# SwiGLU on a 8192 x 8192 matrix: both one-row tiles moved to the end of the tile list

## The chip, the cores and the metric

The kernel runs on one core of a Trainium2 chip. The metric is the device time of one execution in microseconds (us), as the median of several runs. The execution that the profiler recorded has a time of its own, the span, which is a little shorter than the time of a run, because a run also counts what lies around the profiled instructions.

## What is computed

The input x is 8192 x 8192 in float32. Each row is cut into a left half a and a right half b, and the output, 8192 x 4096 in float32, is a times silu(b):

```python
a, b = np.split(x, 2, axis=-1)
silu_b = b / (1 + np.exp(-b))
return a * silu_b
```

So 268.44 MB are read and 134.22 MB are written, and each input element is used once.

## The kernel before

The 8192 rows are cut into tiles that cover all 128 partitions. A tile has one or two rows per partition: a one-row tile covers 128 rows of x (a load of 4096 KB and a store of 2048 KB), a two-row tile covers 256 (a load of 8192 KB and a store of 4096 KB). The list `rows` (line 26) sets the tiles: before, one row, then 31 tiles of two rows, then one row, 33 tiles in all with numbers 0 to 32 (`last` is 32).

There are three buffers, `slots` (line 32). Tile i lives in slot i % 3, and everything happens in place: the load fills the slot, ScalarE (ACT) overwrites b by silu(b) (line 62), VectorE (DVE) multiplies it with a and writes the product into the front of the slot (line 64), and the store sends the front of the slot to the output. The next load into the same slot, tile i + 3, waits until the store of tile i has landed.

The order is written out by hand (lines 83 to 97): loads 0, 1 and 2 are issued at once; then for each tile its arithmetic, its store, and the load of tile i + 3. Each engine carries out its own instructions in this order, which matters for SyncE (SP): it issues all 33 loads (line 51) and the last three stores, so its list ends with load 31, load 32, store 30, store 31, store 32. An instruction at the head of that list that waits holds back all behind it. The other stores (line 77) are issued by ACT, except stores 17 and 19, which GpSimd (POOL) issues (lines 74 to 76). Each issuing engine has its own DMA queue: q1 for SP, q10 for ACT, q0 for POOL. All three queues are served by the same 16 DMA engines, and each of the 16 carries 8 partitions of every transfer, one packet per partition: 64 KB for a two-row load, 32 KB for a one-row load or a two-row store, 16 KB for a one-row store.

The arithmetic of a tile is one ACT and one DVE instruction over both rows, with exceptions at the ends: `by_halves` (line 69) cuts a one-row tile into two halves of its columns (tiles 0 and 32), and tiles 1 and 31 are worked row by row (lines 88 to 90), so that DVE can begin on the first part while ACT does the second.

Of the kernel before, what the change touches and what calls it, by code (L numbers as in the profile page):

```python
# [1 line left out]

# [4 lines left out]

_SILU = mybir.ActivationFunctionType.Silu


@with_exitstack
def kernel(
    ctx: ExitStack,
    tc: tile.TileContext,
    x: bass.AP,
    out: bass.AP,
):

    nc = tc.nc  # L20
    N, M = x.shape
    half = M // 2
    P = nc.NUM_PARTITIONS
    BUFS = 3

    rows = [1] + [2] * (N // P // 2 - 1) + [1]
    first = [sum(rows[:i]) * P for i in range(len(rows))]
    last = len(rows) - 1

    pool = ctx.enter_context(tc.tile_pool(name="sbuf", bufs=1))  # L30
    ctx.enter_context(tc.manual_schedule())
    slots = [pool.tile([P, 2 * M], x.dtype, name=f"slot{s}") for s in range(BUFS)]
    loads, gates, prods, stores = ([[] for _ in rows] for _ in range(4))
    newest = {}

    def in_dram(t, i, width):

        return bass.AP(t.tensor, first[i] * width, [[rows[i] * width, P], [1, rows[i] * width]])

    def follows_from_others(inst, i, current, earlier):  # L40


        targets = [t for kind in current for t in kind[i]]
        targets += [t for kind in earlier for j in range(i % BUFS, i, BUFS) for t in kind[j]]
        for t in targets:
            if t is not newest.get(inst.ins.engine):
                tc.declare_no_dep(inst.ins, t.ins, reason="ordered by the other waits")
        newest[inst.ins.engine] = inst

    def load(i):  # L50
        inst = nc.sync.dma_start(  # L51
            out=slots[i % BUFS][:, : rows[i] * M], in_=in_dram(x, i, M)
        )
        follows_from_others(inst, i, [], [loads, gates, prods])
        loads[i].append(inst)

    def swiglu(i, k0, k1, c0=0, cw=half):
        view = slots[i % BUFS].rearrange("p (k s c) -> p k s c", k=2, s=2)
        a = view[:, k0:k1, 0, c0 : c0 + cw]
        b = view[:, k0:k1, 1, c0 : c0 + cw]  # L60
        o = slots[i % BUFS][:, : 2 * half].rearrange("p (k c) -> p k c", k=2)
        gate = nc.scalar.activation(out=b, in_=b, func=_SILU)  # L62
        follows_from_others(gate, i, [], [loads, gates, prods, stores])
        prod = nc.vector.tensor_mul(out=o[:, k0:k1, c0 : c0 + cw], in0=a, in1=b)  # L64
        follows_from_others(prod, i, [loads], [loads, gates, prods, stores])
        gates[i].append(gate)
        prods[i].append(prod)

    def by_halves(i):
        for c0 in range(0, half, half // 2):  # L70
            swiglu(i, 0, 1, c0, half // 2)

    def store(i):
        eng = nc.scalar if i < last - 2 else nc.sync
        if i % 2 and last // 2 <= i < last // 2 + 4:
            eng = nc.gpsimd
        inst = eng.dma_start(  # L77
            out=in_dram(out, i, half), in_=slots[i % BUFS][:, : rows[i] * half]
        )
        follows_from_others(inst, i, [loads, gates], [loads, gates, prods, stores])  # L80
        stores[i].append(inst)

    for i in range(BUFS):
        load(i)
    for i in range(last):
        if i == 0:
            by_halves(i)
        elif i in (1, last - 1):
            swiglu(i, 0, 1)
            swiglu(i, 1, 2)  # L90
        else:
            swiglu(i, 0, rows[i])
        store(i)
        if i + BUFS <= last:
            load(i + BUFS)
    by_halves(last)
    store(last)


# [1 line left out]
_INS = ['x']  # L101
_OUTS = [((8192, 4096), 'float32')]


# [23 lines left out]
```

## Time and profile before

| | |
|---|---|
| median of 3 runs | 934.87 us (934.86 to 935.44) |
| span of the profiled execution | 933.16 us, so 1.71 us of the median lie outside it |
| DVE, ACT busy | 278.7 us, 226.8 us |
| mean DMA rate over the span | 432 GB/s |
| tile 0: load landed, store issued | 12.93 us, 19.42 us |
| tile 32: load landed, store issued, store landed | 908.10 us, 915.45 us, 932.28 us |

Times in the trace are counted from the start of the span. "Issued" is when an engine hands a DMA to its queue, "landed" is when the last of the 16 DMA engines has reported it done. The trace also holds a record for each packet: queue, start, duration and size. The number of the DMA engine is not in the record, but the packets of one engine follow each other so closely that they can be strung together.

### The profile page before, as it was taken

How to read it: one execution, taken by the hardware profiler on the slowest of the kernel's cores; microseconds unless marked ns; L12 is line 12 of the kernel's file. 1: busy time of each engine (PE TensorE's matmuls, PEld its weight loads, DVE VectorE, ACT ScalarE, POOL GpSimd, SP SyncE). 2: the span in 40 equal slices, each digit the busy share in tenths (PEclk: the TensorE clock that was granted, in tenths of full speed). 3: DMA queues.
4: the chain of work that ended last, by engine and by line, in shares of the span. 5: the costliest groups of instructions: out<-in, count | busy, mean ns of one | idle time of the engine just before them, and what ended most of it. 6: DMA issues, size and time to landing. Idle time of an engine off the chain costs nothing.

```text
span 933.2 us, 220 instructions
## 1 busy us (share of the span) xinstructions
DVE 278.7 (30%) x37; ACT 226.8 (24%) x38; POOL 1.4 (0%) x6
## 2 busy tenths in 40 slices
DVE  1312333123331233312333113332133321333242
ACT  2331133311333203332033320233202332023330
POOL 0000000000000000000000000000000000000000
DMA  9999999999999999999999999999999999999998
GB/s 405 405 449 431 423 451 444 409 444 433 444 427 434 442 410 448 428 433 442 434 421 441 445 417 444 428 454 427 420 457 405 449 427 428 448 445 409 427 444 388
DMA packets 9505, 402.67 MB, mean 432 GB/s; under 512 B 1056, under 2 KB 1056, under 8 KB 1056
## 3 DMA queue, kind: packets, MB, share of 16 engines
q1 hardware_dynamic: 5184, 278.92, 69.1%
q10 hardware_dynamic: 4032, 115.35, 28.6%
q0 software_dynamic: 288, 8.39, 2.1%
q14 instruction: 1, 0.01, 0.0%
HBM read 268.44 MB, written 134.22 MB: 431 GB/s over the span
## 4 chain that ended last, share of the span: by engine, by line
DMA 72%; DVE 11%; ACT 8%; issue 6%; another core or an unknown queue 1%; DVEq 0%; POOL 0%; SPq 0%; ACTq 0%; POOLq 0%
DMA slot<-in_x_dram 40%; DMA out_dram<-slot 32%; DVE slot L64 11%; ACT slot L62 8%; DVEq L123 0%; POOL out_dram L77 0%; SPq L51 0%; ACTq L77 0%; DVEq L64 0%; POOLq L123 0%
## 5 line engine op out<-in xcount | busy, mean ns | idle before, releaser
L64 DVE TENSOR_TENSOR slot<-slot 128x8192 f32<-128x8192 f32 (+2 forms) x37 | 278.7, 7539 | 636.7 <-ACT slot L62 636.5
L62 ACT ACTIVATE slot<-slot 128x8192 f32<-128x8192 f32 (+2 forms) x37 | 225.6, 6107 | 684.3 <-DMA slot<-in_x_dram 684.3
L77 POOL DMA_DIRECT2D out_dram<-slot x2 | 1.2, 600 | 568.9 <-DVE slot L64 568.9
L62 ACT ACT_TABLE_LOAD x1 | 1.3, 1283 | 0.7 <-PEq L112 0.7
L112 POOL MEMSET const-bfloat16-1.0<- 128x1 bf16 x1 | 0.1, 102 | 0.0
L112 POOL MEMSET const-float32-0.0<- 128x1 f32 x1 | 0.1, 99 | 0.2 <-issue 0.2
L112 POOL MEMSET const-float32-1.0<- 128x1 f32 x1 | 0.1, 99 | 0.0
L112 POOL MEMSET const-uint8-127<- 128x1 uint8 x1 | 0.1, 99 | 0.0
## 6 DMA issues: line engine op xcount, KB each, us to landing
out_dram<-slot ACTq DMA_DIRECT2D x27, 4096.0 KB, 33.5
slot<-in_x_dram SPq DMA_DIRECT2D x2, 4096.0 KB, 13.6
out_dram<-slot POOLq DMA_DIRECT2D x2, 4096.0 KB, 34.4
out_dram<-slot SPq DMA_DIRECT2D x2, 4096.0 KB, 20.4
out_dram<-slot ACTq DMA_DIRECT2D x1, 2048.0 KB, 28.1
out_dram<-slot SPq DMA_DIRECT2D x1, 2048.0 KB, 16.8
slot<-in_x_dram SPq DMA_DIRECT2D x31, 37.7
```

The source lines that it names most:

```text
L62: gate = nc.scalar.activation(out=b, in_=b, func=_SILU)
L64: prod = nc.vector.tensor_mul(out=o[:, k0:k1, c0 : c0 + cw], in0=a, in1=b)
L77: inst = eng.dma_start(out=in_dram(out, i, half), in_=slots[i % BUFS][:, : rows[i] * half])
L112: nc = _bacc.Bacc("TRN2", target_bir_lowering=False, num_devices=1)
```

## The change

The list of tiles becomes 31 tiles of two rows followed by two tiles of one row. The number of tiles stays 33, and so do the slot of each tile number, the engine that issues each load and store, and the waits between them. Tile 0 becomes a two-row tile and is worked row by row instead of by halves; tiles 1 and 2 stay as they are in size; tile 30, still of two rows, is worked row by row instead of in one instruction; tile 31 has one row and is worked in one instruction; tile 32 stays a one-row tile by halves. Each tile from 1 to 31 begins 128 rows later in x. ACT and DVE carry out 37 instructions of arithmetic each, before and after: 29 of 128x8192, 4 of 128x4096 and 4 of 128x2048 elements before; 28, 7 and 2 after.

```diff
-    rows = [1] + [2] * (N // P // 2 - 1) + [1]
+    rows = [2] * (N // P // 2 - 1) + [1, 1]
     first = [sum(rows[:i]) * P for i in range(len(rows))]
     last = len(rows) - 1
...
     for i in range(last):
-        if i == 0:
-            by_halves(i)
-        elif i in (1, last - 1):
+        if i in (0, 1, last - 2):
             swiglu(i, 0, 1)
             swiglu(i, 1, 2)
         else:
```

## Prediction, made before the result was known

> **What bounds the kernel now.** I read first the page's totals and its 40 slices.
>
> ```profile
> span 933.2 us, 220 instructions
> ## 1 busy us (share of the span) xinstructions
> DVE 278.7 (30%) x37; ACT 226.8 (24%) x38; POOL 1.4 (0%) x6
> ...
> DMA  9999999999999999999999999999999999999998
> ...
> DMA packets 9505, 402.67 MB, mean 432 GB/s; under 512 B 1056, under 2 KB 1056, under 8 KB 1056
> ```
>
> DVE and ACT work for under a third of the span, while the DMA engines are busy in every slice, the first and the last too. Next, the table of stretches, for the time between the first packet and the last:
>
> ```profile
> core 0: us, DVE busy (x) ACT busy (x) POOL busy (x), PEclk, DMA share, GB/s
> 2.00:932.00 930.00, 278.68 (x37) 225.58 (x38) 1.20 (x2) 1.00 1.00 432
> ```
>
> The DMA share is 1.00 over 930 us. Strung together by engine, the packet records confirm it: the first starts at 1.74 us, the last ends at 931.95, and between them the 16 engines together show one pause above 0.03 us, of 0.34. The span is therefore 1.74 us of start, 930.2 us of DMA engines at work without a hole, and 1.2 us behind the last packet. What matters is that packets are never lacking, not when a given tile is computed.
>
> Third, the end, where a hole could open. The chain of waits, from store 28 on, and SP's instructions in order of time:
>
> ```profile
> 830.95 33.04 DMA out_dram<-slot
> 863.98 0.02 issue
> 864.00 34.39 DMA slot<-in_x_dram
> 898.39 0.02 issue
> 898.41 3.63 ACT slot L62
> 902.04 0.02 issue
> 902.06 4.44 DVE slot L64
> ```
>
> ```profile
> 864.00 29.33 SPq L51 DMA_DIRECT2D slot<-in_x_dram  x2
> 893.38 22.40 SPq L77 DMA_DIRECT2D out_dram<-slot  x3
> ```
>
> Store 28 lands at 863.98 and load 31 follows, landing at 898.39. In SP's rows the second load, load 32, is issued at 893.00 (864.00 + 29.33, less the 0.33 it takes), when store 29 has landed (892.98). The three stores behind it run from 893.38 to 915.78. Store 30's product was ready at 888.85 (DVE: 880.16 + 8.69); it stood 4.5 us behind the waiting load. That cost nothing, as load 31 still had packets in q1.
>
> **The change part by part.**
>
> *Bytes and packets.* Per DMA engine both kernels carry 31 x 8 load packets of 64 KB (2.418 us each), 2 x 8 of 32 KB (1.213), 31 x 8 store packets of 32 KB (1.213) and 2 x 8 of 16 KB (0.611): 599.7 + 19.4 + 300.8 + 9.8 = 929.7 us, plus some 0.6 us of end markers. The change orders them anew; their sum changes by 0.
>
> *Arithmetic.* DVE goes from 29 x 8.692 + 4 x 4.426 + 4 x 2.286 = 278.9 to 28 x 8.692 + 7 x 4.426 + 2 x 2.286 = 278.9, ACT likewise. Nothing changes, and with a third of the span busy it would stay hidden.
>
> *The start.* Load 0 is 4096 KB more, 8 packets per engine of 2.418 instead of 1.213: its landing goes from 12.93 to 12.93 + 9.64 = 22.6. Tile 0 then takes 3.6 (ACT, first row) + 2 x 4.43 (DVE) + 0.1 = 12.6 instead of 6.5, so store 0 is issued at 35.2 instead of 19.42. The cover is the three loads queued at once, now 24 packets of 2.418 per engine, which last until 1.74 + 0.7 + 58.0 = 60.4 even without store 0. That store enters some 1 us after its issue (the first load: issued 0.74, first packet 1.74) and one packet further on, near 38.7. From there its 8 packets alternate with load packets, 2.418 + 1.213 = 3.63 us a pair, and end near 67.7; load 3 is issued near 69. Load 2 lasts until 71.4, and store 1 has stood in q10 since 56 (load 1 landed at 43.3, plus 12.6). Neither queue runs dry: 0 us. If this cover failed, load 3 would miss some 2 us.
>
> *The phase that the start leaves.* When a store has ended on an engine, the next load enters only after landing, semaphore and issue; I count how many packets of the load before it are left then. In the trace of before it is 3 or 4 at first, 2 from 196 us on, and 3 from 571 us on, where the POOL store's later entry gave loads a free turn. In the changed kernel it starts at 1: store 1 ends near 96.8 and load 3 near 100.4. The stores have more lead in return: store 2 is issued at 88, 9 us before store 1 lands (4.5 before). So POOL's stores 17 and 19 can run beside the ACT store ahead of them, which ends each of them a turn earlier against the loads, and the count should rise by about one at either. I take 2 to 3 at the end and keep 1 as a bound.
>
> *The end.* Before, one engine does this: store 28 ends at 861.17; three pairs end load 30 at 872.06; five store packets alternate with five of load 31; store 29 ends at 890.20; three 64 KB packets, 7.25 us, are left until 897.45. After, load 31 has 32 KB packets, so the alternation is one to one. With count c, 8 - c packets of each pass in turn after load 30, and c packets of 1.213 us remain when store 29 ends there: cover 3.64, 2.43 or 1.21 us for c = 3, 2, 1. Against it stands the turnaround to load 32's first packet. Engines end store 29 within 0.6 us of each other (890.17 to 890.79) but for one, 2.43 later, half of which is 1.21 with the smaller packets; landing follows the last marker by 0.35, SP's issue by 0.02, the first packet by 1.0. That is 2.0 us without a late engine, 2.6 with one. The hole is then 0 (c = 3), 0 to 0.2 (c = 2), 0.8 to 1.4 (c = 1); restarting after a pause costs 0.7 more, by the first packets of the kernel (1.9 instead of 1.213). So 0, 0 to 0.9, or 1.5 to 2.1 us. The restart after so short a pause is not in the trace: between 0 and 0.7 (nothing makes it a gain), I take half for a near miss.
>
> Behind load 32 no hole follows. Store 30 is in q1 at once and brings 9.7 us more work. One-row tile 31 needs 3.62 + 4.43 = 8.1 us from its landing, at most 2 us before load 32 starts, and has 19.4 us of packets as cover. Tile 32 needs 1.9 + 4.6 = 6.5 from its landing, with store 30 and store 31 (9.7 + 4.85) as cover. The last store is 16 KB packets as before, and 1.2 us follow.
>
> *Sum.* 0 (bytes) + 0 (start) + 0 to 0.9 (end) makes 933.2 to 934.1 for the span; I take 933.4. With the 1.7 us outside the span: 935.1, against a median of 934.87.
>
> **A rule weighed.** Row: two filled queues alternate record by record, 64 KB, 32 KB, 64 KB (861.18, 863.59, 864.81). The Trainium skill, "DMA: Bandwidth & Descriptors", section "Queues, rings and completion order", says an engine drains a whole packet of typically 9 to 17 descriptors from one queue before it switches. If that packet were a transfer's whole share, load 31 could be gone before store 29 ends; the trace disagrees for these transfers.
>
> **The rivals.**
>
> 1. *A hole behind store 29* (slower). SP can't issue store 30, ready before store 29 lands, past the waiting load 32, so only load 31's rest fills the engines. It decides from a count of 1 with a late engine: 2.1 us, 937.0. For it: the start gives 1, and one engine is late in most of before. Against it: the POOL stores raise the count, and the phase before was at 3 here. Chance 0.13.
> 2. *Queues drained transfer by transfer* there: load 31 leaves no cover, so the full turnaround of 2.0 and a restart of 0.7 are lost: 2.7, 937.5 (the rule above would do this). Against it: the alternation in all of before. Chance 0.03.
> 3. *Fill decides*: the chain of waits moves with tile 0's later landing, 9.6 us: 944.5. Against it: no DMA pause in 930 us. Chance 0.02.
> 4. *A shorter drain* (faster). After the last load only 4096 + 2048 + 2048 KB of stores are left instead of 10240 KB, 2048 KB or 4.85 us less: 930.0. Against it: the same bytes are then moved earlier on engines with no idle time to take them. Chance 0.03.
>
> That the change doesn't do what it says is excluded by the built order of instructions: tile 0 is 128x16384 elements, tiles 31 and 32 are 128x8192, and the waits are the same.
>
> **How the numbers follow.** The forecast, with count 1 and no late engine (1.5 us, 936.4) counted in, has 0.79; the rivals have 0.13, 0.03, 0.02 and 0.03. A measurement can tell about 0.2%, 1.9 us. Faster: rival 4, 0.03. Slower: rivals 1 to 3, 0.18. Same: 0.79. The range reaches from 934.3 (the forecast less the spread of the runs) to 937.2 (rival 1); rivals 2 to 4 are left out.
>
> **What would show it.** Right: DMA share 1.00 from 2 to 932 us, load 0 landing near 22.6, store 0 issued near 35, store 30 issued right behind load 32, the last store landing at 932 to 933. Rival 1: a pause in q1 on most engines between load 31's last packet and load 32's first, and a last landing shifted by just that. Wrong altogether: 64 KB packets longer than 2.418 us somewhere, or a pause in the first 100 us.

## The result, and the profile after

The changed kernel takes 938.29 us (median of 15 runs, 935.27 to 939.95), the kernel before 935.23 us in the same comparison (15 runs, 934.86 to 937.32). The ratio is 1.0026 with a 95% interval of 1.0018 to 1.0033: slower by 0.26%, some 2.4 us by the ratio and 3.1 by the medians. It lies above the predicted range. The profiled execution took 937.14 us, 1.15 less than the median, with a span of 935.4 against 933.16 before. First its page:

```profile
span 935.4 us, 221 instructions
## 1 busy us (share of the span) xinstructions
DVE 278.9 (30%) x37; ACT 226.8 (24%) x38; POOL 1.4 (0%) x6
...
DMA  9999999999999999999999999999999999999998
...
DMA packets 9505, 402.67 MB, mean 430 GB/s; under 512 B 1056, under 2 KB 1056, under 8 KB 1056
```

The number of packets, the bytes and the busy time of the engines are what they were; only the mean rate fell, from 432 to 430 GB/s. The table of stretches for the time between the first packet and the last (columns as before) looks almost harmless:

```profile
2.00:934.00 932.00, 278.87 (x37) 225.52 (x38) 1.20 (x2) 1.00 1.00 431
```

The DMA share is again 1.00, now over 932 us instead of 930. A share of 1.00 therefore does not say that no time was lost: a packet's record mostly runs on until the next one begins (the two times agree within 0.01 us), so a pause can hide inside a longer packet. I compared each packet's length with what its size usually takes (2.414, 1.209 or 0.607 us from start to start) and added up the excess, as a mean over the 16 engines:

| where | before | after | what stands there |
|---|---|---|---|
| first packet | 0.76 | 0.70 | start of the kernel |
| 20 to 45 us | 0.73 | 1.36 | load 1's packets while store 0, the first transfer in q10, enters |
| 900 to 915 us | 0 | 1.46 | load 32 |
| last packet's end, first and last engine | 931.33, 931.95 | 933.15, 934.15 | |

So 1.46 us were lost at the end and 0.6 more than before at the start; the latest engine, which lags the mean a little more, adds 0.1. That makes the 2.2 us between the two spans. The rest of the 3.1 us between the medians lies in executions slower than the profiled one, which this trace doesn't show. The chain of waits shows the end (start, length, what):

```profile
875.25 26.07 DMA out_dram<-slot
901.32 0.02 issue
901.34 13.76 DMA slot<-in_x_dram
915.10 0.02 issue
915.12 1.92 ACT slot L62
917.04 0.02 issue
917.07 2.29 DVE slot L64
```

Store 29 is issued at 875.25 and lands at 901.32; 0.02 us later load 32 goes out, and lands after 13.76 us. Before, load 31 stood in this place; load 32 lay behind it in a filled queue. SP's instructions in order of time:

```profile
879.58 22.09 SPq L51 DMA_DIRECT2D slot<-in_x_dram  x2
901.72 20.20 SPq L77 DMA_DIRECT2D out_dram<-slot  x3
```

Load 32 and store 30 are issued 0.38 us apart, as before. What differs is the queue at that moment. One engine's packets in q1 (KB at start, in us; s is a store packet of q10, | the end marker of a transfer):

```
before  887.78 64 | s-end 890.20  890.20 64  892.62 64  895.03 64 | 897.45 32  898.66 32 ...  905.92 32 | 907.13 32
after   899.04 32 | s-end 900.25  900.25 32  901.46 32 | 902.68 32  904.05 32 ...  910.10 32  912.00 32 | 914.02 32
```

On this engine, before, load 31 still had 7.25 us of packets when store 29 ended, and load 32 was issued (893.00) 4.45 us before they ran out. After, it had 2.43 us, and load 32 came (901.34) only 1.34 us before the queue was dry. Its first packet then took 1.37 us, and its last two 1.90 and 2.01 instead of 1.21. Over the 16 engines the first packet lost 0.25 us and the last two 1.21: the greater part of the loss does not stand where the queue ran dry, but 7 to 9 us behind it.

### The profile page after: what moved, and what is told of

It is laid out like the page before. It is cut to its first block, busy times and chain, and to the rows that moved or that the text cites. A ratio compares the mean times of both kernels' runs of the same rounds, so it can differ in the third digit from the quotient of the medians.

```text
span 935.4 us, 221 instructions
## 1 busy us (share of the span) xinstructions
DVE 278.9 (30%) x37; ACT 226.8 (24%) x38; POOL 1.4 (0%) x6
## 4 chain that ended last, share of the span: by engine, by line
DMA 78%; DVE 10%; ACT 8%; another core or an unknown queue 2%; DVEq 0%; issue 0%; SPq 0%; ACTq 0%
DMA slot<-in_x_dram 41%; DMA out_dram<-slot 37%; DVE slot L64 10%; ACT slot L62 8%; DVEq L121 0%; SPq L51 0%; ACTq L77 0%; DVEq L64 0%
## 5 line engine op out<-in xcount | busy, mean ns | idle before, releaser
L64 DVE TENSOR_TENSOR slot<-slot 128x8192 f32<-128x8192 f32 (+2 forms) x37 | 278.9, 7539 | 642.7 <-ACT slot L62 642.4
```

## The experiments

Theory A: the loss at the end comes from q1 running dry while load 32 waits for store 29, and some 0.6 us come from the start. Rivals: the start costs everything (B), the turn from loads to stores in one queue costs it, or the shifted rows do (C). All times are medians, each set against the kernel before measured again beside it.

**e1, the changed kernel again.**

> The changed kernel once more, for a second profile. Theory A (a hole at the end, before load 32, plus some 0.6 us at the start) and rival B (the start costs it all) both expect about 938.3 us. A expects in the trace packet time lost around 901 to 914 us, 1.5 us or more, in every execution, and more of it in a slower one; B expects the end whole and the loss in the first 50 us.

938.25 us (937.17 to 938.86) against 935.07, ratio 1.0027 [1.0018, 1.0037]. The second profile has the same places: 1.2 us at 35 to 45 us, 1.51 us at 902 to 914. One engine ends at 935.06 while most others end near 933.4, so the span is 936.3 instead of 935.4: the latest engine sets the time. B falls.

**e2, no wait: tile 32 in the free half of tile 31's slot.**

```diff
+    def slot(i):
+        return i % BUFS if i < last else (last - 1) % BUFS
+    def base(i):
+        return 0 if i < last else M
...
-            out=slots[i % BUFS][:, : rows[i] * M], in_=in_dram(x, i, M)
+            out=slots[slot(i)][:, base(i) : base(i) + rows[i] * M], in_=in_dram(x, i, M)
```

(and the same places in the arithmetic and the store of tile 32)

> Tile 32 is loaded into the free upper half of tile 31's slot, so load 32 no longer waits for store 29 and is issued right behind load 31. A: the hole at the end goes, the start's 0.6 us stay: 935.4 to 936.4 us. B: the start is untouched, so the time stays near 938.3. C (the last packets of a load stall whenever a store follows them in the same queue): 0.3 us better at most, 938.

936.31 us (935.95 to 936.87), ratio 1.0007 [0.9997, 1.0016]. Nearly 2 of the 3 us are gone. SP's rows:

```profile
879.62 0.87 SPq L57 DMA_DIRECT2D slot<-in_x_dram  x2
901.14 19.60 SPq L87 DMA_DIRECT2D out_dram<-slot  x3
```

Both loads are now issued within 0.87 us, store 30 as late as ever. No packet from 880 us on is longer than its size says, although loads are followed by stores in q1 as in the changed kernel. The turn from loads to stores is not the cause; the wait on a queue about to run dry, which this edit takes away, can be. What is left, 1.2 us by the medians (the interval of the ratio just takes in no difference) and 1.0 by the spans, stands at 36 to 45 us: a mean of 1.46 us, and up to 2.1 on three engines.

**e3, store 30 on ScalarE's queue.**

```diff
-        eng = nc.scalar if i < last - 2 else nc.sync
+        eng = nc.scalar if i < last - 1 else nc.sync
```

> Store 30 is issued by ScalarE on its own queue instead of by SyncE behind load 32; load 32 still waits for store 29. A: the short pause before load 32's first packet stays (some 0.3 us), the loss at the handover from load 32 to store 30 goes, since the two queues alternate: about 937. B: no change, 938.3. C: the handover is gone, 937.

939.88 us, ratio 1.0043 [1.0027, 1.0059]: slower than the changed kernel itself, which none of the three expected. All instructions from 895 us on:

```profile
901.17 0.33 SPq L51 DMA_DIRECT2D slot<-in_x_dram  x1
901.38 0.34 ACTq L77 DMA_DIRECT2D out_dram<-slot  x1
...
912.52 18.74 SPq L77 DMA_DIRECT2D out_dram<-slot  x2
924.45 3.71 ACT L62 ACTIVATE slot<-slot 128x2048 f32<-128x2048 f32 x2 [16.42 <-DMA slot<-in_x_dram]
```

Store 30 had waited only some 0.3 us behind load 32 (its product is ready at about 901.05). On a queue of its own it shares the engines with load 32, which lands at 924.43 instead of 915.10; store 32 is issued at 930.9, and the engines stand idle for 3.7 us between the end of store 31 and it. Load 32 loses 1.0 us in its first two packets here and nothing in its last ones. So store 30 behind load 32 in SP's list is not the fault: taken out of it, the kernel is slower.

**e4, the end alone.**

```diff
-    rows = [2] * (N // P // 2 - 1) + [1, 1]
+    rows = [1, 1] + [2] * (N // P // 2 - 2) + [1, 1]
...
-        if i in (0, 1, last - 2):
+        if i == 0:
+            by_halves(i)
+        elif i in (2, last - 2):
```

> Two one-row tiles at each end (34 tiles): the end has the sizes of the changed kernel, the start is as light as before. A: the end's loss without the start's: 1.5 to 2.5 us over the kernel before, 936.7 to 937.7. B: the start is light, so no loss: 934.5 to 935.5.

938.57 us (935.72 to 941.18), ratio 1.0027 [1.0012, 1.0043]. Without the heavy first load the loss at the end is there, 1.6 us at 902 to 914, so B fails again. The time overshoots what A expected: in its profile one engine ends 2 us behind most others, and it has been behind since 103 us, so this run bears out A by its trace more than by its time.

**e5, the wait covered: store 30 in two rows, one of them ahead of load 32.**

```diff
+        if i == last - 2:
+            swiglu(i, 0, 1)
+            store_row(i, 0)
+            load(last)
+            swiglu(i, 1, 2)
+            store_row(i, 1)
+            continue
```

> Store 30 is cut into its two rows, and the first one (2048 KB, 4.85 us of packets) is issued by SyncE ahead of load 32, which still waits for store 29. A (the loss at the end comes from queue q1 running dry while load 32 waits): the wait stays and is covered, so about the time of the half-slot run, 935.9 to 936.9 us. Rival (the loss belongs to the turn from loads to stores in one queue): there are more such turns, so 938.3 or more.

936.84 us, ratio 1.0016 [1.0007, 1.0025]. SP's rows:

```profile
879.59 0.33 SPq L51 DMA_DIRECT2D slot<-in_x_dram  x1
896.66 0.35 SPq L84 DMA_DIRECT2D out_dram<-slot  x1
901.35 0.33 SPq L51 DMA_DIRECT2D slot<-in_x_dram  x1
901.77 0.43 SPq L84 DMA_DIRECT2D out_dram<-slot  x1
```

Load 32 waits just as long (901.35), but 2048 KB of a store (4.85 us) lie ahead of it: the excess at the end falls from 1.46 us to 0.05 (the half microsecond over e2 goes with one engine that ends 1.5 us behind most others). The same loss was removed in two ways, by taking the wait away and by covering it: the wait on a dry queue is its cause.

**e6, a lighter start on top of e2.** Tile 0's load and store are cut into rows:

```diff
+    load_row(0, 0)
+    load_row(0, 1)
...
+    swiglu(0, 0, 1)
+    store_row(0, 0)
+    swiglu(0, 1, 2)
+    store_row(0, 1)
```

> The half-slot kernel (no wait of load 32 on store 29), and tile 0's load and store are each cut into two rows, so that the first row lands near 12.9 us and its product is stored near 21. A with a start loss from the late first store: both losses gone, 935.0 to 935.5 us. Rival (the rest of the loss comes from the shifted rows, or from somewhere in between): 936.3, as with the half slot alone.

937.10 us, ratio 1.0016 [1.0007, 1.0025]: no gain. The pauses at 20 to 45 us are 1.03 us instead of 1.46, but the two small stores take until 72.76 to land, load 3 waits for both, q1 runs dry near 70.5, and 1.0 us is lost at 75 to 83. The edit brought in the fault that it was to show the absence of; on the start it decides nothing.

**e7 and e8, no store from GpSimd**, in the changed kernel and in the one before:

```diff
-        if i % 2 and last // 2 <= i < last // 2 + 4:
-            eng = nc.gpsimd
```

> The changed kernel with stores 17 and 19 issued by ScalarE instead of GpSimd. A: the count of load packets left when a store ends stays at 1 up to the end instead of rising, so load 32's wait finds 1.2 us less cover: 939 to 940.5 us. Rival (GpSimd's stores have no part in it): 938.3.

> The kernel before, with stores 17 and 19 issued by ScalarE. A: the count stays at 2, the cover before load 32 is 2 packets of 64 KB, 4.8 us, against a turnaround of up to 3.8: no hole, 934.7 to 935.4 us. Rival (the GpSimd stores by themselves cost or save time): outside that.

e7: 937.83 us (937.68 to 938.52), ratio 1.0026 [1.0015, 1.0037]. SP's rows:

```profile
881.83 20.93 SPq L51 DMA_DIRECT2D slot<-in_x_dram  x2
902.81 20.31 SPq L75 DMA_DIRECT2D out_dram<-slot  x3
```

In the trace A's step is there: one load packet instead of two is left at the end of store 29, load 32 is issued at 902.43, 0.45 us before the queue is dry, and the loss grows from 1.46 to 2.45 us. The span is 936.6, against 935.4 and 936.3 for the changed kernel. The step is all in load 32's first packet (1.34 us instead of 0.25); its last two lose 1.1 as ever. The median, though, is not higher, so the price in time was not confirmed; the scatter of the latest engine is as large as the effect. e8: 935.25 us, ratio 0.9999 [0.9991, 1.0008], as A expected.

**e9, tile 30 in one piece.**

```diff
-        if i in (0, 1, last - 2):
+        if i in (0, 1):
```

> The changed kernel with tile 30 worked in one ACT and one DVE instruction instead of row by row, so store 30 is ready at about 904.2 us, 2.9 us behind load 32's issue instead of 0.38. Theory A1 (the second pause, in load 32's last packets, comes from two DMAs handed to a dry queue back to back): the first pause stays, the second goes, about 937.0 us. Rival A2 (it follows from load 32 entering a dry queue, whatever comes behind it): 938.3 as the changed kernel.

937.88 us, ratio 1.0024 [1.0015, 1.0034]. Store 30 is issued at 904.83, 3.7 us after load 32, and the pauses are the same two, 0.27 and 1.16 us. A1 falls: it is not the closeness of the two issues. Working tile 30 by rows costs and brings nothing that can be seen.

**e10, the kernel before on shifted rows.**

```diff
-    first = [sum(rows[:i]) * P for i in range(len(rows))]
+    first = [N - P] + [sum(rows[1:i]) * P for i in range(1, len(rows))]
```

> The kernel before with its first tile taken from the last 128 rows of x and every other tile 128 rows earlier, so that tiles 1 to 31 work on the very rows that tiles 0 to 30 have in the changed kernel; sizes, order and waits are those of before. A: rows don't matter, 934.8 to 935.5 us. Rival C (the shifted rows cost the rest that the half slot left): about 936.3.

935.23 us, ratio 0.9999 [0.9990, 1.0008], and the pauses of before (0.65 at 20 to 35 us, none at the end). C falls: which rows a tile holds does not matter.

**e11, q10 used before store 0**, on top of e2:

```diff
+    warm = pool.tile([P, 128], x.dtype, name="warm")
+    nc.scalar.dma_start(out=warm[:, :], in_=bass.AP(x.tensor, 0, [[M, P], [1, 128]]))
```

> The half-slot kernel, and ScalarE issues one small load (64 KB in all, into a tile that nothing reads) at the very start, so that queue q10 has been used before store 0 comes. Theory S1 (the start's pause is the first use of q10): the pause at 36 to 45 us shrinks, about 935.6 us. Rival S2 (any queue that takes up work after being empty pauses the engines, and a light first use doesn't help): 936.3, as the half-slot kernel alone.

935.93 us (935.62 to 936.47), ratio 0.9998 [0.9986, 1.0011], against e2's 1.0007 [0.9997, 1.0016]; by the medians it is 0.7 us above the kernel before, e2 1.2. The pause at 36 to 45 us is 0.95 us instead of e2's 1.46. That points to S1, but weakly: the intervals overlap, the same start shows anything from 1.06 to 1.46 us in seven profiles (after, e1, e2, e3, e5, e7, e9), and 0.95 is still above the 0.64 to 0.73 of the start of before (before, e8, e10). It is a part of the start's cost at most.

**e12, e2's end with e4's start.**

> The half-slot end with two one-row tiles at the start instead of a two-row one (34 tiles). Against the end-alone run only the wait of load 32's successor on a store is gone; against the half-slot run only the start is lighter. A (a hole at the end and a heavier start, each on its own): both are gone, 935.0 to 935.8 us. Rival (the sizes at the end cost time even without the wait): 936.3 or more.

936.69 us (935.08 to 940.40), ratio 1.0013 [0.9999, 1.0027]. In the profile no packet at the end is longer than usual and the pauses of the start are 0.6 us; 13 of the 16 engines end by 931.7, as before, but the last at 933.4. One lagging engine again sets the time. The pauses went as A expected, but the median did not: it is in the rival's range. The rival's reason does not fit the trace, though. The late engine fell behind in mid-run, from 0.5 to 1.5 us behind the median engine between 190 and 395 us, long before the small tiles at the end. What costs e12 its time is not settled.

## Why the prediction was wrong

*Bytes, packets, arithmetic: 0.* Right. Packets, bytes and DVE's 278.9 us are as forecast.

*The start: 0.* The course was right: load 0 landed at 22.60 (forecast 22.6), store 0 was issued at 35.26 (35.2), load 3 at 69.62 (near 69), and q1 did not run dry. But the entry of store 0 was costed as a change of place alone. In the trace 1.36 us are lost there against 0.73 before, on average and more on some engines; 1.21 of the 1.36 stand in load 1's last packet, and so do 0.58 of the 0.73. The 0.73 was in the trace of before, hidden in the lengths of packets, where a search for pauses between records could not find it. e2, which leaves the start alone, still has a span 1.0 us above before's. Part of it may go when q10 has been used before (e11); why the rest is larger than before was not settled.

*The count of packets left: 1 at the start, raised by GpSimd's stores to 2 to 3.* Right: near 97 us one packet is left on 13 of the engines and two on three, at the end two on 13 and three on three, and e7 shows that without those stores it stays at one on most. Of before the prediction read one engine only: on 12 or more of the 16 the count was three from store 1 to the end, not two.

*The end: a hole of 0 to 0.9, and behind load 32 no hole.* The first half held; the second is the step that failed. The place, the cover (2.43 us) and the landing were as forecast, and so, nearly, was the turnaround. I took 1.0 us from issue to first packet and 0 to 0.7 for the restart. If a packet's start is counted as its end less its usual length, load 32's first packet began 1.8 to 2.1 us after the issue (the mean, in each profile of the table, over the engines on which it was late). The kernel's first load has the same figure, 1.9 us from issue, so the 0.7 belonged into the sum in full. With 1.9 the prediction's own sum for a count of two is 0.6 + 0.35 + 0.02 + 1.9 - 2.43 = 0.4 us; 0.25 was lost. But for what follows the sum had nothing. Load 32's last two packets took 1.2 us longer than usual, and store 30's packets began late by as much:

| run | load 32 issued | load 31's last packet ends (mean) | lost in load 32's first packet | lost in its last two |
|---|---|---|---|---|
| after | 901.34 | 903.06 | 0.25 | 1.21 |
| e1 | 901.29 | 902.90 | 0.33 | 1.22 |
| e4 (loads 33, 32) | 901.13 | 902.64 | 0.40 | 1.27 |
| e7 | 902.43 | 902.97 | 1.34 | 1.12 |
| e9 | 901.11 | 902.95 | 0.27 | 1.18 |

e7 parts the two. Its queue had 0.5 us left at the issue instead of 1.7, and the first loss grew by 1.1 us, as the prediction's mechanism has it; the second stayed. Both are gone when the wait is gone (e2) or covered (e5), and before, where load 32 was issued 4.45 us ahead, there is neither. So a load that enters a queue run dry brings on both, but why the second stands in its last packets stays open. The Trainium skill, "DMA: Bandwidth & Descriptors", section "Latency and other measured facts", gives about 0.6 us to the first byte for DMAs on the sync and scalar path. The runs here show 1.0 us from issue to the first record at the kernel's start, and 1.8 to 2.1 to the first packet in a queue run dry; the measurement decides.

*The rivals.* Rival 1 named the place. Its hole was there, but at a count of two and with 0.25 us, within the forecast's own range; the 1.2 us behind it were in none of the rivals. That 938.29 lies near its 937.0 and rival 2's 937.5 is therefore chance. In e7, where the count is one on most engines, the hole is 1.34 us, between the 0.8 and 2.1 that the prediction had for it. SP's order, which I named as its reason, had little part (0.3 us, and e3 is slower without it). Rival 2 (transfer by transfer) did not occur: packets alternate until 899. Rivals 3 and 4 did not either: the later first tile cost 0.6 to 1 us and not 9.6, and the smaller rest behind the last load brought nothing.

## What to carry to other kernels

In a kernel whose DMA engines never rest, a transfer that waits for a landing must be issued well before its queue runs dry. Here 4.3 us ahead was enough (e8) and 1.7 was not (the changed kernel, both as means of the engines); making the last load before it smaller took the cover away. To cost such a wait, add the extra length of the first packet to the time from issue to its record, and do not take the hole ahead of that packet for the whole loss: here nearly five times as much stood behind it. A DMA share of 1.00 does not exclude a pause; compare the lengths of packets of one size.

## What the runs showed of the hardware

The time lost around an empty queue does not stand only where the queue is empty. Load 32's first packet was up to 0.8 us too long in four profiles of the table (0.7 to 2.1 in e7), and 1.1 to 1.3 us more appear some 8 us later in its last two packets, in all five. This goes with the dry queue (e2, e5), not with what is issued behind (e9), and not with every entry into a dry queue: in e3, where store 30 shared the engines from another queue, the last packets lost nothing. At the start the loss has the same place: when store 0 enters the empty q10, it stands in the last one or two packets of load 1 (all of the 1.36 us in after and of the 0.95 in e11, 0.58 of 0.73 in before). Why it appears there was not found.

The 16 engines carry the same bytes, but single engines end 1 to 2 us behind (e1: 935.06 against 933.4; e12: 933.4 against 931.5), and the latest sets the time. In e1 that engine was behind from load 1 on, where it lost 2.4 us against a mean of 1.2; in e12 it fell behind in mid-run. The changed kernel's runs spread over 4.7 us, while most of the runs of the kernel before lie within 2.
